# A decoder trunk's gate and up blocks: a third sum made by an accumulating transfer, another order of the products, 29 arena tiles, and norms in halves

## The chip, the core and the metric

The kernel runs on one core of a Trainium2 chip, as one program with a single launch. The metric is the device time of an execution in microseconds. TensorE (PE in the profile) multiplies, VectorE (DVE), ScalarE (ACT) and GpSimd (POOL) do elementwise work, SyncE (SP) issues loads. The times of three runs are given, and one further execution was taken with the hardware profiler.

## The reference

A trunk of two layers on `x` of 512 tokens and 1024 channels in float32. Each layer adds half a gated feed-forward network (FFN), a token mixer, and half an FFN again; a last RMS norm closes the trunk:

```python
def swiglu(h, w_gate, w_up, w_down):
    return (jax.nn.silu(h @ w_gate) * (h @ w_up)) @ w_down
...
    for layer in range(DEPTH):
        x = x + 0.5 * swiglu(rmsnorm(x, ffn_norm[layer, 0]), ffn_w_gate[layer, 0],
                             ffn_w_up[layer, 0], ffn_w_down[layer, 0])
...
        x = x + y.astype(x.dtype)
        x = x + 0.5 * swiglu(rmsnorm(x, ffn_norm[layer, 1]), ffn_w_gate[layer, 1],
                             ffn_w_up[layer, 1], ffn_w_down[layer, 1])
    return rmsnorm(x, final_norm)
```

`y` is latent attention in the first layer and an mLSTM in the second. An FFN takes 1024 channels to 2816 and back, so four pairs of gate and up matrices are multiplied.

## The kernel before, in words

The program has six phases: `f0` (FFN), `a` (attention), `f1`, `f2`, `m` (the mLSTM), `f3`. Everything stays in SBUF; only weights are loaded.

**Products of split numbers.** Every float32 operand is written as the sum of a high and a low part in the format that TensorE multiplies at full speed, and a product takes three matmuls: high by high, high by low, low by high. A weight tile of 128 x 1024 (512 KB) is split by two instructions: ACT casts it to `whi` (L161), DVE subtracts that from it to get `wlo` (L162). There are three buffers each of `whi` and `wlo`; `weights` splits up to AHEAD = 2 tiles ahead of the product that asks for one.

**A gate and up stage.** The 22 column blocks of an FFN's gate and up matrices are taken in pairs. The first NB = 2 pairs are multiplied directly (`plain`, L193 to L195). The other nine pairs, the blocks of this document, go through `seven`: a two-by-two scheme in which seven products of half-size operands do the work of eight. Its products are numbered 1 to 7. Each has a weight tile of its own, made from the four quarters a11, a12, a21, a22: product 1 takes a11, product 5 takes S1 = a22 + a21, product 6 takes s2 = a11 + S1, product 7 takes s3 = a21 + a11, product 2 takes a12, product 3 takes s4 = s2 + a12, product 4 takes a22. (The layout stores the quarters with signs so that all of these are sums.) The other operand, `b1h`, `b1l` to `b7h`, `b7l`, is made from the normed activations once a stage (`normed_blocks`). A product is 24 matmuls (L440 to L442) into one of the banks `px`, `py`, `pz`, `pw`. DVE and ACT combine the banks to `u2`, `u4`, `c12` and apply the gate (`finish`).

**How the sums are made before.** S1 and s3 are made by two transfers: SP loads one quarter (L122), then POOL issues a transfer that adds the other quarter onto the tile as it lands (L125). S1 lies in a tile of the arena, a pool of ARENA = 28 tiles of 128 x 1024 that also holds the operands `b1h` to `b7l`, the activations `act` and the `slab` tiles; s3 lies in one of three `raw` tiles. s2 and s4 are made by DVE at L149: s2 = a11 + S1 into a new arena tile, then, once s2 has been split, s4 = a12 + s2 into the same tile. a12 also has an arena tile.

**What sets the order.** `plan_ffn` writes down the order of the weight tiles, `load_later` the order of the loads. A tile's load is issued up to LOADS = 3 ahead in that list (`load_ahead`), and it waits until a buffer of its pool is free. Each engine runs its instructions in program order; the sum for the next block's s2 stands between DVE's other work wherever `value` is called for it.

**Behind the stage.** `down_plain` and `down_seven` multiply by `w_down` in the same ways; there a12 is already added by a transfer onto a sum that has been split (L166). At the end of `down_seven` eight `norm_tile` calls square each tile of `x` (ACT, L256) and add the squares (DVE, L257); in the last FFN TensorE sums them over the partitions (`rstd`, L263). `mlstm` interleaves the products of eight heads with the chain that makes their normalisers (`factors`, the `rows` matmuls at L199).

Of the kernel before, what the change touches and what calls it, by code (L numbers as in the profile page):

```python
# [26 lines left out]
F32 = mybir.dt.float32  # L27
# [7 lines left out]
P = 128  # L35
T = 512
# [8 lines left out]
DC = 3  # L45
ARENA = 28
LOADS = 3
# [17 lines left out]
class Trunk:  # L65
# [73 lines left out]
    def value(self, src):  # L139

        if src[0] == "load":
            self.first = max(self.first, src[1] + 1)
            self.load_to(self.first)
            return self.loaded[src[1]]
        if src[1] not in self.made:
            _, n, a, b, new = src[:5]
            a, b = self.value(a), self.value(b)
            t = self.duo("sum", F32) if new else b
            self.nc.vector.tensor_tensor(out=t, in0=a, in1=b, op=ALU.add)  # L149
            self.made[n] = t  # L150
        return self.made[src[1]]

    def split_pieces(self, pieces, ahead=True):
# [6 lines left out]
        for a, b in pieces or [(0, n)]:  # L160
# [3 lines left out]
            yield  # L164
        if src[0] == "sum" and len(src) == 6:
            self.nc.gpsimd.dma_start(out=raw, in_=self.row(*src[5]), accum_op=ALU.add)  # L166
        if ahead:
# [77 lines left out]
    def norm_tile(self, d):  # L245
# [3 lines left out]
        self.norm_square(d)  # L249

    def square(self, acc, src, first):
        if first:
            self.nc.scalar.activation(acc, src, AF.Square)
        else:
            sq = self.t512("sq")
            self.nc.scalar.activation(sq, src, AF.Square)  # L256
            self.nc.vector.tensor_tensor(out=acc, in0=acc, in1=sq, op=ALU.add)  # L257

    def rstd(self, acc, n, times=None):

        st = self.ps2.tile([P, T], F32, name="st", tag="st")
        for q in range(NT):
            self.nc.tensor.matmul(st[:, q:q + 1], acc[:, q * P:(q + 1) * P], self.ones[:, 0:1], start=True, stop=True)  # L263
        ms = self.small.tile([P, NT], F32, name="ms", tag="ms")
# [30 lines left out]
    def begin(self, gcol):  # L295
# [16 lines left out]
        self.ident = cst[:, 0:P]  # L312
        self.ones = cst[:, P:2 * P]
        self.mask = cst[:, 2 * P:3 * P]
        self.maskT = cst[:, 3 * P:4 * P]
        self.invf = cst[:, 4 * P:4 * P + 1]
        self.sign = cst[:, 4 * P + 1:4 * P + 2]
        self.sel = cst[:, 4 * P + 2:4 * P + 10]
        self.norm_begin(gcol)
# [14 lines left out]
    def constants(self):  # L334
        nc = self.nc
        self.onesr = self.const.tile([P, P], F32R, name="onesr")
        nc.scalar.copy(out=self.onesr, in_=self.ones)
        self.pick = self.const.tile([P, P + 40], F32R, name="pick")
# [16 lines left out]
    def normed_blocks(self, rb):  # L355
# [26 lines left out]
        t3 = self.duo("t3", F32)  # L382
        v.tensor_tensor(out=t3, in0=b22, in1=b12, op=ALU.subtract)
        v.tensor_tensor(out=b12, in0=b11, in1=b12, op=ALU.subtract)
        yield
        v.tensor_tensor(out=b11, in0=t3, in1=b11, op=ALU.add)
        split(6, b11)
        yield
        split(5, b12)
        yield  # L390
        split(7, t3)
        yield
# [32 lines left out]
    def seven(self, outs):  # L425
# [25 lines left out]
        u2 = self.t512("u2")  # L451
        nc.scalar.copy(out=u2, in_=bx)
        product(by, 6, True, True)
        v.tensor_tensor(out=u2, in0=u2, in1=by, op=ALU.subtract)
        product(bz, 5, True, False)
        u4 = self.t512("u4")
        v.tensor_tensor(out=u4, in0=u2, in1=bz, op=ALU.add)
        product(bw, 7, True, False)
        v.scalar_tensor_tensor(out=u4, in0=bw, scalar=-1.0, in1=u4, op0=ALU.mult, op1=ALU.subtract)  # L459
# [103 lines left out]
    def down_seven(self, slabs):  # L563
# [64 lines left out]
        for c in range(4):  # L628
            product(bw, 4, c, first=False)
        add(1, 0, bw, -0.5)  # L630
        for d in range(4, 8):
            self.norm_tile(d)

    def plan_ffn(self, f):
# [4 lines left out]
        for j in range(NU - NB):  # L639
            a11, a21, a22, a12 = (("wgs", f, j, i) for i in range(4))  # L640
            s1 = self.load_later(a22, pool="sum", plus=a21)
            b11 = self.load_later(a11)
            s3 = self.load_later(a21, plus=a11)
            a11 = b11
            a12 = self.load_later(a12, pool="raw")
            a22 = self.load_later(a22)
            n = 2 * (f * NU + j)
            s2 = "sum", n, a11, s1, True
            s4 = "sum", n + 1, a12, s2, False
            for p, src in ((1, a11), (6, s2), (5, s1), (7, s3), (2, a12), (3, s4), (4, a22)):  # L650
                self.plan(("st", p), W, src)
# [4 lines left out]
        for c in range(5):  # L656
            if c < 4:
                a11, a21, a22, a12 = (("wds", f, i, c) for i in range(4))
                s1 = self.load_later(a22, pool="sum", plus=a21)
                a11 = self.load_later(a11)  # L660
                sums.append(("sum", ("dn", f, c), a11, s1, True, a12))
                for p, src in ((1, a11), (6, sums[c]), (5, s1)):
                    self.plan(("dn", p), W, src)
            if c:
                self.plan(("dn", 3), W, ("sum", ("dn", f, c - 1)))
        for c in range(4):
# [273 lines left out]
    def mlstm(self, next_gain):  # L940
# [255 lines left out]
        def out(part, i):  # L1196
            self.mix_out("wo2", part, i, ys)
# [15 lines left out]
        for p in range(3):  # L1213
# [13 lines left out]
            if p == 0:  # L1227
                for f in pending:
                    f()
            decay(a + 2)  # L1230
            if p == 2:
                for f in pending:
                    f()
            conv(p + 2) if p < 2 else out(0, 0)
            decay(b + 2)
# [101 lines left out]
def layout(i):  # L1337
# [60 lines left out]
    sel = np.concatenate([np.eye(32, 8), np.eye(96, 8)]).astype(np.float32)  # L1398
    a["cst"] = c(np.concatenate([ident, ones, later, later.T, invf, sign, sel], 1))
    return a  # L1400
# [20 lines left out]
```

## Time and profile before

| what | value |
|---|---|
| median of three runs | 1874.31 us (1873.33 to 1880.12) |
| the profiled execution's own time | 1876.21 us |
| its span, in which the rows below lie | 1874.4 us |
| TensorE, busy | 1821.4 us, 12240 matmuls |
| DVE, busy | 1457.4 us |
| ACT, busy | 932.2 us |
| POOL, busy | 131.3 us |
| moved from HBM | 261.68 MB, 141 GB/s over the span |

All rows come from the profiled execution. A row of a timeline begins with its start and its length in us; `L149` is a line of the kernel, `out<-in` gives the program's names, and brackets hold the idle time ahead of an instruction and what ended it. A DMA row is the issue of a transfer; how long it takes to land is given apart.

### The profile page before, as it was taken

How to read it: one execution, taken by the hardware profiler on the slowest of the kernel's cores; microseconds unless marked ns; L12 is line 12 of the kernel's file. 1: busy time of each engine (PE TensorE's matmuls, PEld its weight loads, DVE VectorE, ACT ScalarE, POOL GpSimd, SP SyncE). 2: the span in 40 equal slices, each digit the busy share in tenths (PEclk: the TensorE clock that was granted, in tenths of full speed). 3: DMA queues.
4: the chain of work that ended last, by engine and by line, in shares of the span. 5: the costliest groups of instructions: out<-in, count | busy, mean ns of one | idle time of the engine just before them, and what ended most of it. 6: DMA issues, size and time to landing. Idle time of an engine off the chain costs nothing.

```text
span 1874.4 us, 30014 instructions
## 1 busy us (share of the span) xinstructions
PE 1821.4 (97%) x12240; PEld 1668.1 (89%) x12240; DVE 1457.4 (78%) x1903; ACT 932.2 (50%) x1312; POOL 131.3 (7%) x154
## 2 busy tenths in 40 slices
PE   9999999999999999999999999999998999999996
PEld 7999989978887999889989998997876779999896
DVE  7867799767767777788697769778878778777885
ACT  5444445566544444435444445446767544444452
POOL 1000001000000010001000000100000000000010
PEclk9999999999999999999999999999998999999998
DMA  6575667321124585577467564743221246755762
GB/s 202 146 207 141 166 185 176 129 84 63 46 69 134 148 218 144 135 189 169 135 167 204 146 178 152 185 127 113 79 68 56 68 125 162 220 137 147 197 161 91
DMA packets 74922, 265.73 MB, mean 142 GB/s; under 512 B 8336, under 2 KB 9360, under 8 KB 74784
## 3 DMA queue, kind: packets, MB, share of 16 engines
q1 hardware_dynamic: 57312, 200.30, 31.5%
q0 software_dynamic: 17472, 63.51, 19.4%
q8 instruction: 96, 1.57, 0.3%
q14 instruction: 42, 0.34, 0.1%
HBM read 261.68 MB, written 2.10 MB: 141 GB/s over the span
## 4 chain that ended last, share of the span: by engine, by line
PE 70%; DVE 9%; issue 8%; DMA 8%; ACT 3%; POOL 1%; POOLq 0%; DVEq 0%; SPq 0%; ACTq 0%
DMA sum<-in_wgs 7%; PE y L193 4%; PE y L194 4%; PE y L195 4%; PE pw L442 3%; PE pw L440 3%; PE pw L441 3%; PE pz L442 3%; PE pz L440 3%; PE pz L441 3%; PE px L440 3%; PE px L441 3%; PE px L442 3%; DVE wlo L162 2%; PE py L442 1%
## 5 line engine op out<-in xcount | busy, mean ns | idle before, releaser
L161 ACT CAST whi<-raw 128x1024 fp32r<-128x1024 f32 (+2 forms) x314 | 322.0, 1027 | 401.5 <-issue 100.1
L162 DVE TENSOR_TENSOR wlo<-raw,whi 128x1024 fp32r<-128x1024 f32 (+2 forms) x314 | 374.5, 1193 | 94.9 <-ACT whi L161 93.5
L161 ACT CAST whi<-sum 128x1024 fp32r<-128x1024 f32 x172 | 179.7, 1047 | 237.3 <-PE pz L441 74.6
L162 DVE TENSOR_TENSOR wlo<-sum,whi 128x1024 fp32r<-128x1024 f32 x172 | 209.8, 1220 | 58.6 <-ACT whi L161 58.2
L149 DVE TENSOR_TENSOR sum<-raw,sum 128x1024 f32<-128x1024 f32 x88 | 107.2, 1219 | 68.5 <-DMA sum<-in_wgs 57.2
L440 PE MATMUL pw<-b4h,whi 128*128 128x256 f32 x288 | 83.0, 288 | 6.3 <-DVE u L459 6.3
L442 PE MATMUL pw<-b4h,wlo 128*128 128x256 f32 x288 | 83.2, 289 | 4.4 <-DVE wlo L162 4.4
L442 PE MATMUL pz<-b3h,wlo 128*128 128x256 f32 x288 | 82.0, 285 | 5.2 <-DVE wlo L162 5.2
L440 PE MATMUL py<-b6h,whi 128*128 128x256 f32 x288 | 82.6, 287 | 3.0 <-ACT whi L161 3.0
L442 PE MATMUL py<-b6h,wlo 128*128 128x256 f32 x288 | 82.8, 287 | 2.4 <-DVE wlo L162 2.3
L441 PE MATMUL pw<-b4l,whi 128*128 128x256 f32 x288 | 82.6, 287 | 0.0
L441 PE MATMUL py<-b6l,whi 128*128 128x256 f32 x288 | 82.5, 286 | 0.0
L441 PE MATMUL pz<-b3l,whi 128*128 128x256 f32 x288 | 82.0, 285 | 0.0
L440 PE MATMUL pz<-b3h,whi 128*128 128x256 f32 x288 | 81.9, 284 | 0.0
L441 PE MATMUL pz<-b5l,whi 128*128 128x256 f32 x288 | 81.5, 283 | 0.0
L441 PE MATMUL px<-b1l,whi 128*128 128x256 f32 x288 | 81.4, 283 | 0.0
L441 PE MATMUL px<-b2l,whi 128*128 128x256 f32 x288 | 81.3, 282 | 0.0
L441 PE MATMUL pw<-b7l,whi 128*128 128x256 f32 x288 | 81.3, 282 | 0.0
L440 PE MATMUL px<-b1h,whi 128*128 128x256 f32 x288 | 81.3, 282 | 0.0
L440 PE MATMUL pz<-b5h,whi 128*128 128x256 f32 x288 | 81.3, 282 | 0.0
L440 PE MATMUL pw<-b7h,whi 128*128 128x256 f32 x288 | 81.2, 282 | 0.0
L440 PE MATMUL px<-b2h,whi 128*128 128x256 f32 x288 | 81.2, 282 | 0.0
(419 smaller groups left out, 6116.4 us busy)
## 6 DMA issues: line engine op xcount, KB each, us to landing
raw<-in_wgs SPq DMA_DIRECT2D x144, 512.0 KB, 4.2
sum<-in_wds POOLq DMA_DIRECT2D x48, 512.0 KB, 6.7
raw<-in_wds SPq DMA_DIRECT2D x48, 512.0 KB, 3.3
sum<-in_wgs SPq DMA_DIRECT2D x36, 512.0 KB, 4.8
sum<-in_wgs POOLq DMA_DIRECT2D x36, 512.0 KB, 6.4
raw<-in_wgs POOLq DMA_DIRECT2D x36, 512.0 KB, 5.9
sum<-in_wds SPq DMA_DIRECT2D x32, 512.0 KB, 4.5
raw<-in_wgc SPq DMA_DIRECT2D x30, 512.0 KB, 3.3
```

The source lines that it names most:

```text
L149: self.nc.vector.tensor_tensor(out=t, in0=a, in1=b, op=ALU.add)
L161: self.nc.scalar.copy(out=hi[:, a:b], in_=raw[:, a:b])
L162: self.nc.vector.tensor_tensor(out=lo[:, a:b], in0=raw[:, a:b], in1=hi[:, a:b].bitcast(F32), op=ALU.subtract)
L193: mm(out, lhs[0], rhs[0], start=start, stop=False)
L194: mm(out, lhs[0], rhs[1], start=False, stop=False)
L195: mm(out, lhs[1], rhs[0], start=False, stop=stop)
L440: mm(out, wh, bh[:, b], start=first and e + k == 0, stop=False, skip_group_check=True)
L441: mm(out, wh, bl[:, b], start=False, stop=False, skip_group_check=True)
L442: mm(out, wl, bh[:, b], start=False, stop=last and e + k == 4, skip_group_check=True)
```

## The change

- In the nine blocks of a gate and up stage s4 is no longer made by DVE. a12 is loaded into a `raw` tile, for product 2 alone; when s2 has been split, POOL issues a transfer that adds a12 from HBM onto the tile of s2 (L167 of the kernel after). A stage has nine more accumulating transfers of 512 KB and nine fewer sums on DVE.
- The order of the products is 1, 7, 6, 5, 2, 3, 4 instead of 1, 6, 5, 7, 2, 3, 4; `normed_blocks` makes the operand of product 7 earlier to match.
- A block uses two tiles of the arena (S1 and s2) and four of the `raw` loads; ARENA is 29. The constants lose their 128 columns of ones, of which one is kept and broadcast.
- The last four norm tiles of each FFN are done in halves of 256 columns: the second half, whose part of `x` is final earlier, inside the loop of product 4; the first half behind it.
- In `mlstm`, for the last pair of heads but one, the first output product is put ahead of the pending squares.

The core of the diff:

```diff
-ARENA = 28
+ARENA = 29
...
         if src[1] not in self.made:
-            _, n, a, b, new = src[:5]
+            _, n, a, b, _ = src
             a, b = self.value(a), self.value(b)
-            t = self.duo("sum", F32) if new else b
+            t = self.duo("sum", F32)
             self.nc.vector.tensor_tensor(out=t, in0=a, in1=b, op=ALU.add)
...
-        if src[0] == "sum" and len(src) == 6:
-            self.nc.gpsimd.dma_start(out=raw, in_=self.row(*src[5]), accum_op=ALU.add)
+        if src[0] == "sum" and len(src) > 2:
+            self.nc.gpsimd.dma_start(out=raw, in_=self.row(*src[4]), accum_op=ALU.add)
...
+    def norm_half(self, d, n):
+
+        t = slice(n * T // 2, n * T // 2 + T // 2)
+        if self.gcol is not None:
+            if self.xg[d] is None:
+                self.xg[d] = self.pair()
+            self.split_to([a[:, t] for a in self.xg[d]], self.x[d][:, t], self.vec(self.gcol + d))
+        self.square(self.acc[:, t], self.x[d][:, t], False)
...
         product(bx, 1, True, False)
         u2 = self.t512("u2")
         nc.scalar.copy(out=u2, in_=bx)
+        product(bw, 7, True, False)
         product(by, 6, True, True)
         v.tensor_tensor(out=u2, in0=u2, in1=by, op=ALU.subtract)
         product(bz, 5, True, False)
         u4 = self.t512("u4")
         v.tensor_tensor(out=u4, in0=u2, in1=bz, op=ALU.add)
-        product(bw, 7, True, False)
...
         for c in range(4):
             product(bw, 4, c, first=False)
+            self.norm_half(4 + c, 1)
         add(1, 0, bw, -0.5)
         for d in range(4, 8):
-            self.norm_tile(d)
+            self.norm_half(d, 0)
...
-            a12 = self.load_later(a12, pool="raw")
-            a22 = self.load_later(a22)
-            n = 2 * (f * NU + j)
-            s2 = "sum", n, a11, s1, True
-            s4 = "sum", n + 1, a12, s2, False
-            for p, src in ((1, a11), (6, s2), (5, s1), (7, s3), (2, a12), (3, s4), (4, a22)):
+            s2 = "sum", ("gu", f, j), a11, s1, a12
+            a12, a22 = self.load_later(a12), self.load_later(a22)
+            for p, src in ((1, a11), (7, s3), (6, s2), (5, s1), (2, a12), (3, s2[:2]), (4, a22)):
                 self.plan(("st", p), W, src)
...
+            conv(p + 2) if p < 2 else out(0, 0)
             if p == 2:
                 for f in pending:
                     f()
-            conv(p + 2) if p < 2 else out(0, 0)
             decay(b + 2)
```

Three places show what the change does to the order of instructions. Lines move by one here and there: the sum at L149 is L150 after the change, the subtraction at L162 is L163, the accumulation at L166 is L167.

**First, DVE in the eighth block of an FFN, where the sum for the ninth block's s2 stands** (`sum_2446` before, `sum_2482` after; its second operand is S1 of the ninth block). Before:

```order
L454 TENSOR_TENSOR u2_2276<-u2_2276,py_2245 128x512
L162 TENSOR_TENSOR wlo_2311<-raw_2177,whi_2310 128x1024
L457 TENSOR_TENSOR u4_2340<-u2_2276,pz_2246 128x512
L162 TENSOR_TENSOR wlo_2344<-sum_2210,whi_2343 128x1024
L149 TENSOR_TENSOR sum_2446<-raw_2314,sum_2282 128x1024
L459 SCALAR_TENSOR_TENSOR u4_2340<-pw_2247,u4_2340 128x512
L162 TENSOR_TENSOR wlo_2376<-raw_2179,whi_2375 128x1024
L447 TENSOR_TENSOR slab_1771<-sg_2372,u4_2340 128x256
```

After:

```order
L476 SCALAR_TENSOR_TENSOR u2_2044<-pw_2012,u2_2044 128x512
L163 TENSOR_TENSOR wlo_2252<-sum_2249,whi_2251 128x1024
L455 TENSOR_TENSOR slab_1771<-sg_2242,u2_2044 128x256
L150 TENSOR_TENSOR sum_2482<-raw_2314,sum_2214 128x1024
L163 TENSOR_TENSOR wlo_2283<-sum_1978,whi_2282 128x1024
L163 TENSOR_TENSOR wlo_2311<-raw_2177,whi_2310 128x1024
L463 TENSOR_TENSOR u2_2280<-u2_2280,py_2246 128x512
L163 TENSOR_TENSOR wlo_2342<-sum_2249,whi_2341 128x1024
```

The sum stood behind the split of the eighth block's product 3, just ahead of the `u4` that reads product 7; it now stands behind the end of the seventh block, ahead of the split of the eighth block's product 5.

**Second, DVE at the start of the third block** (the sum for its s2 is `sum_1024` before and `sum_1063` after, the split of product 6 is `wlo_1027` and `wlo_1066`). Before:

```order
L447 TENSOR_TENSOR slab_819<-sg_1021,c12_1019 128x256
L149 TENSOR_TENSOR sum_1024<-raw_892,sum_860 128x1024
L468 SCALAR_TENSOR_TENSOR u2_854<-pw_825,u2_854 128x512
L162 TENSOR_TENSOR wlo_1027<-sum_1024,whi_1026 128x1024
L447 TENSOR_TENSOR slab_820<-sg_1055,u2_854 128x256
L162 TENSOR_TENSOR wlo_1063<-sum_860,whi_1062 128x1024
L149 TENSOR_TENSOR sum_1024<-raw_991,sum_1024 128x1024
```

After:

```order
L163 TENSOR_TENSOR wlo_1023<-raw_957,whi_1022 128x1024
L455 TENSOR_TENSOR slab_820<-sg_1019,c12_1017 128x256
L476 SCALAR_TENSOR_TENSOR u2_858<-pw_826,u2_858 128x512
L455 TENSOR_TENSOR slab_821<-sg_1056,u2_858 128x256
L150 TENSOR_TENSOR sum_1063<-raw_892,sum_788 128x1024
L163 TENSOR_TENSOR wlo_1066<-sum_1063,whi_1065 128x1024
L163 TENSOR_TENSOR wlo_1097<-sum_788,whi_1096 128x1024
L163 TENSOR_TENSOR wlo_1125<-raw_991,whi_1124 128x1024
```

The second sum (`raw_991` is a12) is gone. The split of product 7 (`wlo_1023`) has come ahead, and the sum for s2 stands behind all work of the block before, directly ahead of the split of s2; the seventh block reads the same, while in most other blocks the sum stands a block earlier.

**Third, POOL's queue from the third block on** (`raw` is s3, `sum` on L125 is S1, on L167 s2 becoming s4). Before:

```order
L125 DMA raw_957<-in_wgs 128x1024
L125 DMA sum_1096<-in_wgs 128x1024
L125 DMA raw_1193<-in_wgs 128x1024
L125 DMA sum_1332<-in_wgs 128x1024
L125 DMA sum_1568<-in_wgs 128x1024
L125 DMA raw_1429<-in_wgs 128x1024
```

After:

```order
L125 DMA raw_957<-in_wgs 128x1024
L125 DMA sum_1028<-in_wgs 128x1024
L167 DMA sum_1063<-in_wgs 128x1024
L125 DMA sum_1264<-in_wgs 128x1024
L125 DMA sum_1500<-in_wgs 128x1024
L125 DMA raw_1193<-in_wgs 128x1024
L167 DMA sum_1299<-in_wgs 128x1024
L125 DMA sum_1736<-in_wgs 128x1024
```

Both begin with s3 of the third block and S1 of the fourth. Before, s3 of the fourth follows; after, s4 of the third block, then S1 of the fifth and of the sixth, and only then s3 of the fourth.

## Rows read from the trace of the kernel before

**Rows 1.** The page, part 1: busy time, share of the span, instructions of each engine.

```profile
PE 1821.4 (97%) x12240; PEld 1668.1 (89%) x12240; DVE 1457.4 (78%) x1903; ACT 932.2 (50%) x1312; POOL 131.3 (7%) x154
```

**Rows 2.** Stretches (us from:to, length, busy per engine, TensorE clock, DMA share): gate/up, one block.

```profile
55.30:249.05 193.75, 185.96 (x1513) 184.53 (x1512) 147.84 (x173) 89.00 (x116) 14.31 (x18) 0.98 0.60 160
610.90:804.20 193.30, 186.21 (x1514) 184.80 (x1513) 148.30 (x174) 88.92 (x115) 13.62 (x16) 0.98 0.61 162
965.80:1153.20 187.40, 183.95 (x1513) 183.13 (x1512) 146.55 (x172) 88.81 (x115) 13.62 (x16) 0.99 0.62 167
1554.00:1740.10 186.10, 183.09 (x1514) 181.83 (x1513) 146.59 (x172) 88.44 (x115) 13.62 (x16) 1.00 0.62 167
1006.53:1026.69 20.16, 20.16 (x171) 20.16 (x169) 16.43 (x21) 10.02 (x13) 2.55 (x3) 1.00 0.86 240
```

**Rows 3.** What TensorE waited for: us in total, times, longest.

```profile
PE pw L440 <- DVE u L459: 6.3, 6, 2.3
PE rows L199 <- ACT pr L205: 5.3, 4, 2.9
PE pz L442 <- DVE wlo L162: 5.2, 2, 3.5
PE pw L442 <- DVE wlo L162: 4.4, 8, 0.6
PE st L263 <- DVE acc L257: 3.9, 1, 3.9
...
PE py L440 <- ACT whi L161: 3.0, 3, 1.6
...
PE py L442 <- DVE wlo L162: 2.3, 3, 0.8
```

**Rows 4.** Timeline of the eighth block of f2, all engines: start us, us, engine, line, operation.

```profile
1112.04 0.33 SPq L122 DMA_DIRECT2D sum<-in_wgs  x1
...
1115.93 0.85 POOL L125 DMA_DIRECT2D sum<-in_wgs  x1 [18.03 <-DMA sum<-in_wgs]
...
1125.80 1.22 DVE L149 TENSOR_TENSOR sum<-raw,sum 128x1024 f32<-128x1024 f32 x1 [6.75 <-DMA sum<-in_wgs]
```

**Rows 5.** Stretch of 4 us after the wait in the same block.

```profile
1129.00:1133.00 4.00, 4.00 (x22) 4.00 (x22) 4.00 (x7) 1.64 (x4) 0.00 (x0) 0.57 0.66 201
```

**Rows 6.** Groups by line and shape: count, busy us, mean ns, idle before and releasers.

```profile
L161 ACT CAST whi<-sum 128x1024 fp32r<-128x1024 f32 x172 | 179.7, 1047 | 237.3 <-PE pz L441 74.6 <-issue 40.2 <-PE dx L582 20.2
L149 DVE TENSOR_TENSOR sum<-raw,sum 128x1024 f32<-128x1024 f32 x88 | 107.2, 1219 | 68.5 <-DMA sum<-in_wgs 57.2 <-PE y L194 8.0 <-DMA raw<-in_wgs 3.3
...
L257 DVE TENSOR_TENSOR acc<-acc,sq 128x512 f32<-128x512 f32 x53 | 36.3, 685 | 1.7 <-ACT sq L256 1.1
...
L447 DVE TENSOR_TENSOR slab<-sg,u 128x256 f32<-128x256 f32 x64 | 26.7, 418 | 4.8 <-ACT sg L446 4.8
```

**Rows 7.** Line 166, the accumulations onto a split sum in the down stage.

```profile
  ACT whi L161: 14.7, 3
...
DMA to landing us min/median/max: 5.3/6.3/8.9
```

**Rows 8.** Line 125, the accumulations behind a load.

```profile
DMA to landing us min/median/max: 5.2/6.6/9.8
```

**Rows 9.** The page, part 6, loads of the seven-blocks: count, KB each, us to landing.

```profile
raw<-in_wgs SPq DMA_DIRECT2D x144, 512.0 KB, 4.2
```

**Rows 10.** The page, part 3, the two queues (SP's q1, POOL's q0): packets, MB, share.

```profile
q1 hardware_dynamic: 57312, 200.30, 31.5%
q0 software_dynamic: 17472, 63.51, 19.4%
```

**Rows 11.** Timeline of DVE at the first block of f0.

```profile
57.58 1.22 DVE L149 TENSOR_TENSOR sum<-raw,sum 128x1024 f32<-128x1024 f32 x1
58.72 0.68 DVE L420 TENSOR_TENSOR gr<-g,rb 128x512 f32<-128x512 f32 x1
```

**Rows 12.** Timeline of DVE behind the last product.

```profile
1856.61 3.08 DVE L257 TENSOR_TENSOR acc<-acc,sq 128x512 f32<-128x512 f32 x4
```

More of the change, by code (lines that the diff above doesn't have):

```diff
@@ L254, in square @@
         else:
-            sq = self.t512("sq")
+            sq = self.t512("sq")[:, :src.shape[1]]
             self.nc.scalar.activation(sq, src, AF.Square)
@@ L262, in rstd @@
         for q in range(NT):
-            self.nc.tensor.matmul(st[:, q:q + 1], acc[:, q * P:(q + 1) * P], self.ones[:, 0:1], start=True, stop=True)
+            self.nc.tensor.matmul(st[:, q:q + 1], acc[:, q * P:(q + 1) * P], self.one, start=True, stop=True)
         ms = self.small.tile([P, NT], F32, name="ms", tag="ms")
@@ L312, in begin @@
         self.ident = cst[:, 0:P]
[L313 to L318, printed above, removed]
+        self.mask = cst[:, P:2 * P]
+        self.maskT = cst[:, 2 * P:3 * P]
+        self.invf, self.sign, self.one = (cst[:, 3 * P + i:3 * P + i + 1] for i in range(3))
+        self.sel = cst[:, 3 * P + 3:3 * P + 11]
         self.norm_begin(gcol)
@@ L336, in constants @@
         self.onesr = self.const.tile([P, P], F32R, name="onesr")
-        nc.scalar.copy(out=self.onesr, in_=self.ones)
+        nc.scalar.copy(out=self.onesr, in_=self.one.broadcast_to([P, P]))
         self.pick = self.const.tile([P, P + 40], F32R, name="pick")
@@ L383, in normed_blocks @@
         v.tensor_tensor(out=t3, in0=b22, in1=b12, op=ALU.subtract)
+        split(7, t3)
+        yield
         v.tensor_tensor(out=b12, in0=b11, in1=b12, op=ALU.subtract)
+        v.tensor_tensor(out=b11, in0=t3, in1=b11, op=ALU.add)
         yield
-        v.tensor_tensor(out=b11, in0=t3, in1=b11, op=ALU.add)
         split(6, b11)
@@ L389, in normed_blocks @@
         split(5, b12)
-        yield
-        split(7, t3)
         yield
@@ L660, in plan_ffn @@
                 a11 = self.load_later(a11)
-                sums.append(("sum", ("dn", f, c), a11, s1, True, a12))
+                sums.append(("sum", ("dn", f, c), a11, s1, a12))
                 for p, src in ((1, a11), (6, sums[c]), (5, s1)):
@@ L664, in plan_ffn @@
             if c:
-                self.plan(("dn", 3), W, ("sum", ("dn", f, c - 1)))
+                self.plan(("dn", 3), W, sums[c - 1][:2])
         for c in range(4):
@@ L1398, in layout @@
     sel = np.concatenate([np.eye(32, 8), np.eye(96, 8)]).astype(np.float32)
-    a["cst"] = c(np.concatenate([ident, ones, later, later.T, invf, sign, sel], 1))
+    a["cst"] = c(np.concatenate([ident, later, later.T, invf, sign, ones[:, :1], sel], 1))
     return a
```

## The prediction, made before the changed kernel was run

> **What bounds the kernel now.** I read the page first, then busy time and clock by stretch, then the waits of the matmul engine, and last the timeline around a few of these waits. TensorE is busy 97% of the span [rows 1], so time can come only from its idle stretches or from stretches at a lower clock. The change works in the four gate and up stages. Nine blocks of seven products stand in each, and a block in which nothing waits takes 20.16 us, 2.88 a product (the last of [rows 2]). Undisturbed, the four stages would take 4 x 9 x 20.16 = 725.8 us; they take 193.75 + 193.30 + 187.40 + 186.10 = 760.6. So **34.8 us** are lost there, and the parts of the change that lie in these stages cannot win more.
>
> What the loss consists of is in TensorE's waits [rows 3]: `pw` on DVE's `u`, `pz` on `wlo` and `pw` on `wlo` make 6.3 + 5.2 + 4.4 = 15.9 us; `py` on `whi` and on `wlo`, 3.0 + 2.3 = 5.3, is the first block of a stage. The rest, about 13.6, is the lower of the two clock levels (1.2 instead of 2.4 GHz) behind such waits and what the waits' records leave out: the stretch after one of them was granted 0.57 over 4 us, so it cost 4 x 0.43 = 1.7 [rows 5].
>
> Why the 15.9 arise is seen in the eighth block of f2 [rows 4]. S1 of the ninth is loaded from 1112.04, POOL issues what is added to it at 1115.93, and the sum at L149, which needs the result, starts only at 1125.80, after DVE has idled 6.75 us. DVE works in order: behind that sum stands the `u` of product 7 (first order excerpt), and TensorE's `pw` waits for it. DVE idles 57.2 us in the whole kernel for such sums [rows 6], most of it hidden.
>
> **The change, part by part.**
>
> *Earlier S1.* A block holds two arena tiles instead of three, and there are 29 instead of 28, so S1 is loaded and accumulated one to two blocks earlier in the queues (third order excerpt). Both S1 terms, the 15.9 of waits and some 7 of the clock behind them, should go. The sum for the ninth block now stands at the start of the eighth, ahead of the split of product 5 (first order excerpt); a late a11 could hold it there, but product 5 is fourth and has slack.
>
> *The DVE sum that goes.* 36 x 1.219 = 43.9 us of DVE work [rows 6] disappear. DVE is at 78% [rows 1], so by itself this is worth nothing; it gives slack to the splits.
>
> *The accumulation that comes.* s4 = s2 + a12 must be made between the end of s2's split and the start of product 3's. Product 3 is sixth and starts 14.4 us into a block; its split has to start about 2 us earlier (a cast of 1.05 and a subtraction as long as the sum, 1.22 [rows 6], less the 0.24 until the third matmul), near 12.35. In an ordinary block s2's split is over 2.3 to 4.5 us into the block (a cast and a subtraction, with up to two more DVE operations ahead), which leaves 8 to 10 us. In the third and seventh block the sum stands late on DVE (second order excerpt), s2's split ends one sum and one or two short operations later, at 5.5 to 6.8, and 5.6 to 6.8 are left. The same kind of accumulation, on a split sum in the down stage, landed in 5.3, 6.3 and 8.9 us (least, median, most), and ACT's cast waited 14.7 us for three of them [rows 7]; those at L125 took 5.2, 6.6 and 9.8 [rows 8]. Per place the cost lies between 0 and 9.8 - 5.6 = 4.2; I take **1.5**, a landing between the median and the most, as these places fall where loads are dense: 8 x 1.5 = 12 us.
>
> The Trainium skill, page "DMA: Bandwidth & Descriptors", section "Anatomy of one DMA — SWDGE (gpsimd) path", fits a transfer issued from GpSimd by 2.0 us + bytes / 436e3, an estimate of 3.2 us for these 512 KB. By it the third sum would be in time in every block, and the time that of rival B. The trace disagrees for accumulating transfers: none landed under 5.2 us [rows 8], and I keep the rows.
>
> *s3 earlier in the block.* Product 7 is now second, and its raw tile is one of four loads a block that share three buffers: the load waits for the split of the previous block's product 2, which begins with the third product, 5.8 us into that block, and is over at about 8.6. The split of 7 has to start by 20.16 + 2.88 + 0.24 - 1.05 - 1.22 = 21.0. So load and accumulation have 12.4 us; the medians need 4.2 [rows 9] + 6.6 [rows 8] = 10.8. I take 0, and count the delay of the fourth block (its accumulation stands behind two of S1, third order excerpt) among the 8 places above. At the top of the rows, 4.2 + 9.8 = 14.0, it would be 1.6 in each of 32 blocks, 51 us.
>
> *The DMA engines.* A plain load keeps all 16 engines busy for 0.315 x 1874.4 / (200.30 / 0.524) = 1.55 us, an accumulating one for 0.194 x 1874.4 / (63.51 / 0.524) = 3.0 [rows 10]. A block had 5 loads and 2 accumulations, 13.7 us; it now has 5 and 3, 16.7 of 20.16: 0.15 more than a share that is 0.60 to 0.62 now [rows 2]. The last block of [rows 2] ran at a share of 0.86 with no wait, so I expect longer landings but no saturation. POOL's own 36 x 0.85 us [rows 4] change nothing at 7% busy.
>
> *The first block of a stage.* Product 6, which waits for a late sum, gets 2.88 us more. But the subtraction for product 7 comes ahead of it on DVE (1.14 from start to start), and so do the two products with `rb`, which stood behind the sum (1.2) [rows 11]. In f0 the sum then runs from 57.58 + 2.34 = 59.9 to 61.1, the cast and the subtraction end at 63.4, and the third matmul of product 6, due at 55.3 + 2 x 2.88 + 0.24 = 61.3, is 2.1 late; before it was some 0.8 more. So 0.8 goes in each of the three stages that wait, and 5.3 - 2.4 = 2.9 stay.
>
> *Norms in halves.* Behind the last product, four squares and adds are half as long. The adds took 3.08 us together [rows 12]; like the ones of 128x256, at 418 instead of 685 ns [rows 6], four take 1.7, and the first square is some 0.2 shorter: **-1.6** in the tail, where `st` waits 3.9 for them [rows 3]. In the other FFNs nothing is listed as waiting for this chain: 0. The other halves lie under product 4.
>
> *The reordered lines of the mLSTM.* The longest wait of `rows` on ACT, 2.9 [rows 3], stands ahead of what moves; -0.3, between 0 and -1. The smaller `cst` and the copy of a broadcast column: 0, under the first loads; some tenths without that cover.
>
> **Sum.** The stages lose 2.9 + 12 + four low-clock stretches of 1.7 (6.8) = 21.7 instead of 34.8: -13.1. With -1.6 and -0.3 this is -15.0. The profiled execution took 1876.2 us, so 1861.2; it lies 1.9 above the median of the three runs, 1874.3, which makes **1859** as the median.
>
> **The rivals.** *B: all of it comes.* Landings stay near 6.6 and no block but the first waits: 2.9 + two low-clock stretches (3.4) = 6.3 lost, -28.5 and -1.9, so 1844. For it speaks the block at 0.86; against it, the 14.7 us that the twin of this accumulation cost the down stage. *C: the waits move.* Little is won if the late sums are met by landings of 8.9, against 6.2 of time: 2.7 x 8 = 21.6, + 2.9 + 6.8 = 31.3 lost, so about 1869; should S1's loads be held by arena tiles after all, so that the change does not do what it says, nearly nothing is won, 1872. *D, slower: s3 is the new bottleneck.* Three accumulations a block share one queue and slow each other; product 7, now second, waits for the one of s3 in most blocks. It decides from 12.4 us on; at 14.0 it costs 51, so the stages lose 51 + 2.9 + 6.8 = 60.7 against 34.8, and the median is 1898. From about 13.5 on (1.1 in each of 32 blocks) the kernel is measurably slower. For it speaks that the accumulation issued at 1115.93, with plain loads beside it, was not in until 1125.8 [rows 4]; against it the median of 6.6.
>
> **How the numbers follow.** About 0.5% of 1874, 9.4 us, can be told from no change. Forecast 0.50 (its own range 1850 to 1868), B 0.10, C 0.22, D 0.18. Faster: 0.43 of the forecast and B, 0.53. Same: the rest of the forecast and most of C, 0.27. Slower: D and a little of C, 0.20. The range takes in B's and C's times and the beginning of D: 1844 to 1886.
>
> **What would show it.** Right: the sum's wait for `sum<-in_wgs` falls from 57 us to under 10; the stages take about 187 us each; TensorE's wait of `pw` for `u` is gone; the new waits are those of `pz` for `whi` or `wlo`, behind accumulations of a12, in the third and seventh block; `st` waits about 2.3. Wrong: `pw` of product 7 waits for its split in many blocks, at DMA shares near 0.9 (D); accumulations of a12 land near 6 and nothing waits for them (B). I would be wrong in kind if DVE still idles for S1.

## The result, and the profile after

The changed kernel is slower: 1936.39 us in the median (1924.75 to 1942.42, 4 runs) against 1877.21 for the kernel before (1873.33 to 1881.25, 4 runs), a ratio of **1.0308** with the 95% interval 1.0247 to 1.0368. The forecast was 1859, the range ended at 1886. Its profiled execution took 1942.4 us, the slowest of the four and 6 us above their median, with a span of 1940.6.

The page, parts 1 and 3, of the kernel after, beside [rows 1, 10]:

```profile
PE 1848.5 (95%) x12240; PEld 1690.5 (87%) x12240; DVE 1416.7 (73%) x1895; ACT 930.6 (48%) x1340; POOL 163.1 (8%) x190
...
q1 hardware_dynamic: 57312, 200.30, 29.5%
q0 software_dynamic: 22640, 82.32, 24.4%
```

DVE is busy 41 us less (36 sums fewer, some short norm halves more) and POOL's queue carries 18.8 MB more, as the diff says. The four gate and up stages, beside [rows 2]:

```profile
55.55:264.20 208.65, 191.60 (x1514) 189.25 (x1513) 139.87 (x166) 88.59 (x116) 22.73 (x27) 0.96 0.69 177
628.70:835.00 206.30, 190.40 (x1513) 188.07 (x1512) 139.82 (x166) 88.72 (x117) 22.27 (x26) 0.97 0.70 179
996.00:1203.05 207.05, 192.83 (x1513) 189.54 (x1512) 138.81 (x165) 86.87 (x115) 22.19 (x26) 0.96 0.69 178
1603.75:1808.90 205.15, 190.16 (x1514) 187.69 (x1513) 140.60 (x167) 88.87 (x117) 22.17 (x26) 0.97 0.71 182
```

They sum to 827.2 us, 101.4 above the 725.8 of undisturbed blocks, where the kernel before lost 34.8. The difference, 66.6, is the whole difference of the two spans (66.2). The DMA share rose by 0.07 to 0.09 only. What TensorE waited for, beside [rows 3]:

```profile
PE pz L448 <- DVE u L466: 24.5, 13, 3.8
PE pw L448 <- ACT whi L162: 13.2, 8, 3.5
PE py L448 <- ACT whi L162: 8.4, 4, 2.9
PE pw L450 <- DVE wlo L163: 7.3, 10, 0.8
PE pz L448 <- ACT whi L162: 5.8, 6, 3.2
...
PE st L273 <- DVE acc L267: 2.8, 1, 2.8
PE py L450 <- DVE wlo L163: 2.3, 4, 1.5
```

The `pw` that waited for `u` is gone, as forecast; in its place stand `pz` (product 3), `pw` on a split (product 7) and a longer `py` (product 6 of the first block). Who is late is seen in the waits of ACT and DVE:

```profile
ACT whi L162 <- DMA raw<-in_wgs: 145.5, 33, 9.0
ACT whi L162 <- DMA sum<-in_wgs: 120.7, 24, 8.3
...
DVE sum L150 <- DMA raw<-in_wgs: 33.4, 18, 4.0
```

DVE's sum no longer waits for S1 at all (57.2 us before [rows 6]). ACT's cast now waits 33 times for an accumulated s3 and 24 times for an accumulated s4. From the starts of the products in the trace (2.88 us apart when undisturbed) the 101.4 divide thus, the stretches at the lower clock behind a wait included (the granted clock of the stages is 0.96 to 0.97, before 0.98 to 1.00): about 43 ahead of product 3 (s4), 36 ahead of product 7 (s3), 18 in the first blocks, 4 elsewhere.

**One late s4.** The third block of f1 began at 675.5. Timelines of POOL, then DVE, ACT and TensorE:

```profile
677.68 0.85 POOL L125 DMA_DIRECT2D sum<-in_wgs  x1 [8.47 <-DMA sum<-in_wgs]
681.79 0.86 POOL L167 DMA_DIRECT2D sum<-in_wgs  x1 [3.27 <-DMA sum<-in_wgs]
682.33 1.19 POOL L125 DMA_DIRECT2D sum<-in_wgs  x1
...
692.01 1.23 DVE L163 TENSOR_TENSOR wlo<-sum,whi 128x1024 fp32r<-128x1024 f32 x1 [3.22 <-ACT whi L162]
693.15 0.68 DVE L466 TENSOR_TENSOR u<-u,pz 128x512 f32<-128x512 f32 x1
...
690.93 1.04 ACT L162 CAST whi<-sum 128x1024 fp32r<-128x1024 f32 x1 [8.31 <-DMA sum<-in_wgs]
...
693.98 0.36 PE L448 MATMUL pz<-b3h,whi 128*128 128x256 f32 x1 [3.77 <-DVE u L466]
```

The accumulation of a12 was issued 6.3 us into the block, between two for S1, and took until 690.83. The cast, the subtraction and then the `u` at L466 follow; only then does TensorE go on, 3.77 us late. L466 reads product 5 out of the bank that product 3 adds to. Product 5 is now fourth instead of third, and DVE's order has that read **behind** the split of product 3:

```
L463 TENSOR_TENSOR u2_1094<-u2_1094,py_1060 128x512
L163 TENSOR_TENSOR wlo_1156<-sum_1063,whi_1155 128x1024
L466 TENSOR_TENSOR u4_1183<-u2_1094,pz_1061 128x512
```

Before, the same read (L457) stood ahead of `wlo`. So a late s4 costs the time of the split and of this read as well.

**One late s3.** Timelines of SP, POOL and ACT around the start of the fifth block of f1:

```profile
711.21 17.57 SPq L122 DMA_DIRECT2D raw<-in_wgs  x4
...
716.98 0.85 POOL L125 DMA_DIRECT2D raw<-in_wgs  x1 [6.67 <-DVE slab L455]
...
726.12 1.04 ACT L162 CAST whi<-raw 128x1024 fp32r<-128x1024 f32 x1 [8.93 <-DMA raw<-in_wgs]
```

The load is issued 9.9 us into the fourth block (which began at 701.3) and lands in 5.2, POOL follows 0.6 later, and the accumulation takes 9.0: 14.8 us, where the prediction had 12.4 to spend.

**The first block.** ACT and DVE in f1:

```profile
627.15 1.05 ACT L162 CAST whi<-raw 128x1024 fp32r<-128x1024 f32 x1 [5.04 <-DMA raw<-in_wgs]
...
628.24 1.23 DVE L163 TENSOR_TENSOR wlo<-raw,whi 128x1024 fp32r<-128x1024 f32 x1 [2.87 <-ACT whi L162]
```

The subtraction of product 7 stands ahead of everything else on DVE and waits 2.87 us for s3 (2.99 in f2, 2.78 in f3, 0.72 in f0); a subtraction and three splits for the operands, the two products with `rb`, the sum and the split of product 6 stand behind it. TensorE's product 6 came 2.90 us late.

The tail did what it should; DVE and TensorE behind the last product, beside [rows 3, 12]:

```profile
1924.22 2.00 DVE L267 TENSOR_TENSOR acc<-acc,sq 128x256 f32<-128x256 f32 x4
...
1926.37 1.79 PE L273 MATMUL st<-cst,acc 128*128 128x1 f32 x8 [2.79 <-DVE acc L267]
```

### The profile page after: what moved, and what is told of

Its sections match the earlier page's. It is cut to its first block, busy times and chain, and to the rows that moved or that the text cites. A ratio compares the mean times of both kernels' runs of the same rounds, so it can differ in the third digit from the quotient of the medians.

```text
span 1940.6 us, 30163 instructions
## 1 busy us (share of the span) xinstructions
PE 1848.5 (95%) x12240; PEld 1690.5 (87%) x12240; DVE 1416.7 (73%) x1895; ACT 930.6 (48%) x1340; POOL 163.1 (8%) x190
## 5 line engine op out<-in xcount | busy, mean ns | idle before, releaser
L162 ACT CAST whi<-raw 128x1024 fp32r<-128x1024 f32 (+2 forms) x314 | 321.5, 1025 | 432.4 <-DMA raw<-in_wgs 145.5
L163 DVE TENSOR_TENSOR wlo<-raw,whi 128x1024 fp32r<-128x1024 f32 (+2 forms) x314 | 374.2, 1193 | 192.8 <-ACT whi L162 192.0
L162 ACT CAST whi<-sum 128x1024 fp32r<-128x1024 f32 x172 | 179.1, 1045 | 293.6 <-DMA sum<-in_wgs 120.7
L163 DVE TENSOR_TENSOR wlo<-sum,whi 128x1024 fp32r<-128x1024 f32 x172 | 209.2, 1220 | 123.5 <-ACT whi L162 123.3
L448 PE MATMUL pz<-b3h,whi 128*128 128x256 f32 x288 | 87.1, 302 | 28.9 <-DVE u L466 24.5
L448 PE MATMUL pw<-b7h,whi 128*128 128x256 f32 x288 | 86.6, 301 | 13.2 <-ACT whi L162 13.2
L450 PE MATMUL pw<-b7h,wlo 128*128 128x256 f32 x288 | 87.0, 302 | 7.3 <-DVE wlo L163 7.3
L150 DVE TENSOR_TENSOR sum<-raw,sum 128x1024 f32<-128x1024 f32 x52 | 63.4, 1220 | 37.8 <-DMA raw<-in_wgs 33.4
L448 PEld LDWEIGHTS pz<-b3h,whi 128*128 128x128 f32 x288 | 58.9, 204 | 32.0 <-issue 27.1
L449 PE MATMUL pw<-b7l,whi 128*128 128x256 f32 x288 | 85.2, 296 | 0.0
L450 PE MATMUL pz<-b5h,wlo 128*128 128x256 f32 x288 | 81.6, 283 | 0.4 <-DVE wlo L163 0.4
L450 PE MATMUL px<-b1h,wlo 128*128 128x256 f32 x288 | 81.2, 282 | 0.0
```

The lines of the kernel that those rows point to most:

```text
L162: self.nc.scalar.copy(out=hi[:, a:b], in_=raw[:, a:b])
L163: self.nc.vector.tensor_tensor(out=lo[:, a:b], in0=raw[:, a:b], in1=hi[:, a:b].bitcast(F32), op=ALU.subtract)
L448: mm(out, wh, bh[:, b], start=first and e + k == 0, stop=False, skip_group_check=True)
L449: mm(out, wh, bl[:, b], start=False, stop=False, skip_group_check=True)
L450: mm(out, wl, bh[:, b], start=False, stop=last and e + k == 4, skip_group_check=True)
```

## The experiments

Theory A: the place of product 7 is at fault, that is, the order of the products. Theory B: the third accumulation overloads the DMA queues. Theory C: S1's loads, now ahead in bursts, delay s4. "Lost" below is the time of the four gate and up stages above 725.8 us in each run's profile; ratios are to the kernel before in the same session. The kernel before itself took 1877 us (median) in the session of the change, 1884 in that of experiments 1 to 4, 1882 in that of 5 to 8, 1879 in that of 9 to 11 and 1883 in that of 12.

**1. The old order, all else as changed.** The three places (the products in `seven`, the plan, the operands) go back:

```diff
...
-            for p, src in ((1, a11), (7, s3), (6, s2), (5, s1), (2, a12), (3, s2[:2]), (4, a22)):
+            for p, src in ((1, a11), (6, s2), (5, s1), (7, s3), (2, a12), (3, s2[:2]), (4, a22)):
...
```

> The changed kernel with the products in the old order 1, 6, 5, 7, 2, 3, 4; the third accumulation and the 29 tiles stay. In the profile of the change the four gate and up stages lose 101 us: about 42 where product 3 waits for s4, 36 where product 7 waits for s3, 24 in the first blocks. Theory A (the place of product 7 is at fault: s3's load and accumulation have 12.4 us, and its split stalls DVE's queue in the first block): s3 gets 5.8 us more, s4 2.9 more, so the stages lose 20 to 35 and the time is 1865 to 1880. Theory B (the third accumulation overloads the DMA queues): the transfers are still there, product 3 and product 7 still wait, 60 us or more are lost, 1900 to 1930.

Measured: **0.9872** (0.9836 to 0.9907), 1862.84 us in the median; 23.9 us lost. That is 1.3% faster than the kernel before, with the third accumulation in place. The stages, then rows of the waits of DVE and ACT (ACT's for s4 stood at 120.7 us, its for s3 at 145.5 and is gone), then TensorE's longest wait in the blocks:

```profile
54.10:243.05 188.95, 183.97 (x1514) 183.13 (x1513) 142.40 (x167) 90.32 (x117) 21.90 (x26) 0.99 0.75 194
605.90:794.85 188.95, 183.91 (x1514) 183.09 (x1513) 141.40 (x166) 89.77 (x116) 21.40 (x25) 0.99 0.75 194
955.85:1140.55 184.70, 182.22 (x1513) 181.57 (x1512) 139.66 (x164) 89.69 (x116) 21.36 (x25) 1.00 0.77 198
1540.80:1727.95 187.15, 183.95 (x1513) 183.12 (x1512) 141.17 (x166) 89.86 (x116) 21.37 (x25) 0.99 0.76 195
```

```profile
DVE sum L150 <- DMA sum<-in_wgs: 33.1, 8, 5.5
...
ACT whi L162 <- DMA sum<-in_wgs: 9.9, 4, 3.7
```

```profile
PE pz L450 <- DVE wlo L163: 10.2, 8, 2.6
```

The DMA share is higher than in the change (0.75 to 0.77), as the same transfers fill less time, and nothing waits for s3. s4 is issued 0.05 us ahead of its block in the median (6.5 into it in the change), so that every s4 has landed by 11.5 us into its block. B falls as the whole cause. What remains are 10.2 us in the first blocks and eight waits of product 3 in the third and seventh blocks, 13.7 us with the clock behind them, all from DVE's sum that still waits for S1 there.

**2. The new order with DVE's sum for s4**, so without the third accumulations:

```diff
...
+            s4 = "sum", ("g4", f, j), a12, s2
-            for p, src in ((1, a11), (7, s3), (6, s2), (5, s1), (2, a12), (3, s2[:2]), (4, a22)):
+            for p, src in ((1, a11), (7, s3), (6, s2), (5, s1), (2, a12), (3, s4), (4, a22)):
...
```

> The changed kernel with s4 made by DVE again (a12 in its raw tile added onto s2's tile), in the new order and with 29 tiles, so without the 36 third accumulations. Theory A: product 7 still waits for s3 and the first blocks are as in the change, the waits of product 3 go: 50 to 60 us lost, 1890 to 1905. Theory B: without the third accumulation loads and accumulations land as before, s3 is in time, 15 to 30 us are lost, 1860 to 1875.

Measured: 1.0089 (1.0058 to 1.0121), 71.8 us lost. The order alone makes the kernel slower than before; the waits for s3 are all there without any third accumulation:

```profile
ACT whi L162 <- DMA raw<-in_wgs: 156.6, 31, 10.2
```

The loss was larger than theory A had put it (50 to 60): product 7 costs about 41 us, 24 of them in the fourth blocks (10 in the change), and about 9 lie at products 6 and 5.

**3. Both undone**, so that only the earlier S1 is left of the change in the stages:

```diff
...
+            s4 = "sum", ("g4", f, j), a12, s2
-            for p, src in ((1, a11), (7, s3), (6, s2), (5, s1), (2, a12), (3, s2[:2]), (4, a22)):
+            for p, src in ((1, a11), (6, s2), (5, s1), (7, s3), (2, a12), (3, s4), (4, a22)):
...
```

> Old order and DVE's sum for s4 both back: what stays of the change in these stages is two arena tiles a block of 29 and a12 in a raw tile, so that S1 is loaded earlier, besides the norm halves and the reordered lines of the mLSTM. If S1's lateness was the cause of the 24 us that the kernel before loses behind its sums (both theories): these go, first blocks lose 10, 10 to 15 in all, 1850 to 1857. If the early S1 only moves the waits to s3 (four raw loads share three tiles): 1870 to 1885.

Measured: 0.994 (0.9916 to 0.9964), 36.0 us lost in a profiled execution of 1876.1 us. The S1 waits did not go: they are the same kind as before, in the third and seventh blocks, and a few of product 5 came, behind sums that wait for a12 or a11; nothing waits for s3. So the third accumulation, in the old order, is what makes 36.0 into 23.9. What is left of the change here loses as much in its profile as the kernel before did in an execution of 1876.2 us, while the ratio makes it 0.6% faster than the kernel before in its own session; what the earlier S1 is worth alone stays open.

**4. The change with 28 tiles.**

```diff
-ARENA = 29
+ARENA = 28
```

> The changed kernel with 28 arena tiles instead of 29, all else as changed. Theory C (S1's loads running two blocks ahead come in a burst at the third and seventh block and delay s4 there): the waits of product 3 in the third and seventh blocks shrink from about 3 us to 1 or less, 1915 to 1925. Theories A and B: S1 is only a little later, the same waits stay, 1930 to 1945.

Measured: 1.0245 (1.0212 to 1.0279), 91.4 us lost. The waits ahead of product 3 did not shrink (TensorE's `pz` on `u`: 36.4 us in 15 cases, 24.5 in 13 in the change). This does not settle theory C, as the edit leaves S1 almost where it was: POOL's queue has the same order in all four stages as in the change, S1 of the fourth block ahead of s4 of the third, S1 of the fifth and sixth ahead of s3 of the fourth. POOL in the third block of f1 (from 669.1):

```profile
670.98 0.85 POOL L125 DMA_DIRECT2D sum<-in_wgs  x1 [8.17 <-DMA sum<-in_wgs]
675.59 0.86 POOL L167 DMA_DIRECT2D sum<-in_wgs  x1 [3.76 <-DVE wlo L163]
676.17 1.15 POOL L125 DMA_DIRECT2D sum<-in_wgs  x1
```

For theory C speaks the first experiment, where S1 of the fourth block comes behind s4 of the third (from 648.2), and S1 of the fifth behind s3 of the fourth:

```profile
650.99 0.85 POOL L167 DMA_DIRECT2D sum<-in_wgs  x1 [8.62 <-DVE wlo L163]
654.82 0.86 POOL L125 DMA_DIRECT2D sum<-in_wgs  x1 [2.98 <-DMA sum<-in_wgs]
```

There s4 of the third and seventh blocks landed in 5.4 us in the median (8.2 in the change), and s3 of the fourth and eighth in 5.3 (7.7). So a part of the loss may lie in S1's earlier place in the queues, which the new order brings with it; no run moved S1 alone, and this stays open.

**5. The kernel before with the norm halves and the mLSTM lines alone.**

```diff
...
             product(bw, 4, c, first=False)
+            self.norm_half(4 + c, 1)
         add(1, 0, bw, -0.5)
         for d in range(4, 8):
-            self.norm_tile(d)
+            self.norm_half(d, 0)
...
```

> The kernel before with only the norm halves and the reordered lines of the mLSTM. The prediction put these at -1.6 and -0.3, a ratio to the kernel before of 0.999; TensorE's wait for the last add falls from 3.9 to about 2.8 us, as it did in the profile of the change. If the halves' extra instructions cost something in the other three FFNs: 1.000 or above.

Measured: 1.000 (0.9983 to 1.0017). TensorE's wait for the last add is 2.8 us instead of 3.9 there too; 1.1 us is less than this comparison can show.

**6. Product 7 third.**

```diff
...
-            for p, src in ((1, a11), (7, s3), (6, s2), (5, s1), (2, a12), (3, s2[:2]), (4, a22)):
+            for p, src in ((1, a11), (6, s2), (7, s3), (5, s1), (2, a12), (3, s2[:2]), (4, a22)):
...
```

> The changed kernel with product 7 third (1, 6, 7, 5, 2, 3, 4), the third accumulation and 29 tiles kept: between the old order, in which nothing waited for s3, and the new one. s3's chain gets 2.9 us more than in the change: 15.3 instead of 12.4. Theory A (a deadline that s3's chain of load, queue and accumulation misses by 1 to 4 us): most of s3's waits go, s4's stay near the 14 us of the old order or a little more, 30 to 50 us are lost in the stages, ratio 0.995 to 1.005. If instead product 7 has to be behind product 5 for another reason (the queue order of DVE), the loss stays near that of the change, ratio 1.02 or more.

Measured: 1.0057 (1.0037 to 1.0077), 55.2 us lost, at or just past the slow edge of what theory A gave. It is between the two orders, but less for s3 than for product 3: product 7 costs about 15 us of these, product 3 about 33. In 15 blocks product 3 starts about 1 us or more late (5.1 at most): product 5 is fourth here too, and the read of `pz` stands behind a split that is late itself, behind a late s4 or behind a sum that waits for S1 or a11. The run also shows two accumulations issued one right behind the other, for S1 and for s4, in f2:

```profile
996.01 0.85 POOL L125 DMA_DIRECT2D sum<-in_wgs  x1 [7.60 <-DMA sum<-in_wgs]
996.55 1.19 POOL L167 DMA_DIRECT2D sum<-in_wgs  x1
```

The first landed after 6.6 us, the second after 10.7.

**7. The change with four raw buffers** and 28 tiles.

```diff
-ARENA = 29
+ARENA = 28
...
-        raw = self.duo(pool, F32) if pool else self.wp.tile([P, W], F32, name="raw", tag="raw")
+        raw = self.duo(pool, F32) if pool else self.wp.tile([P, W], F32, name="raw", tag="raw", bufs=4)
```

(One more raw load is allowed ahead, too.)

> The changed kernel, its new order and third accumulation kept, with four raw buffers instead of three and 28 arena tiles (the run with 28 tiles and three buffers is the base: ratio 1.0245). If s3 is late because its load waits for the buffer of a12, it can now start one split earlier or more, and the waits of product 7 go: ratio 1.00 to 1.01. If it is late because the accumulations land late whenever they are issued: 1.02 or more.

Measured: 1.0155 (1.0124 to 1.0186) against 1.0245 with three buffers, between the two expectations; 72.1 us lost against 91.4. s3's load is issued 9 us earlier, and only two casts still wait for an s3, 2.0 us in all; no product 7 does. That its load waited for the buffer of a12 is shown. But the accumulations of s4 still land 12.1 us into their block in the median (12.7 with three buffers), each now taking 6.8 us instead of 5.5, and product 3 waits 44 us instead of 40:

```profile
PE pz L448 <- DVE u L466: 36.1, 17, 3.8
PE pz L448 <- ACT whi L162: 8.0, 7, 2.0
```

**8. The old order with product 3 last.**

```diff
...
-            for p, src in ((1, a11), (7, s3), (6, s2), (5, s1), (2, a12), (3, s2[:2]), (4, a22)):
+            for p, src in ((1, a11), (6, s2), (5, s1), (7, s3), (2, a12), (4, a22), (3, s2[:2])):
```

> The old order but with product 3 last (1, 6, 5, 7, 2, 4, 3), third accumulation and 29 tiles kept. In the old order with product 3 sixth, eight waits of product 3 for s4 in the third and seventh blocks cost 13.7 us in all. s4 now has 2.9 us more: these waits fall to below 3 us in all unless they move to the next block's first products, 10 us of first blocks stay: 12 to 15 us lost in the stages, ratio 0.980 to 0.984. If s4's landing was not the deadline that was missed: no change, 0.987.

Measured: 0.9965 (0.9944 to 0.9986), 39.8 us lost; a miss. The eight waits did not go but moved to product 4: DVE's sum that waits for S1 stands ahead of the `u` that reads product 7's bank, to which product 4 adds, one product sooner. So in the old order it was not s4 that was late.

**9. The change with product 3 last.**

```diff
...
-            for p, src in ((1, a11), (7, s3), (6, s2), (5, s1), (2, a12), (3, s2[:2]), (4, a22)):
+            for p, src in ((1, a11), (7, s3), (6, s2), (5, s1), (2, a12), (4, a22), (3, s2[:2])):
```

> The changed kernel with product 3 last instead of sixth (1, 7, 6, 5, 2, 4, 3), all else as changed. In its profile s4 had landed 13.2 us into a block in the median, and 20 of 36 came after 12.3, where the cast of product 3 should begin; the latest came at 16.9. Product 3 last puts that point to 15.2. If missing this point is what costs: the 42 us behind product 2 fall to 10 or less, the 36 for s3 and 20 in the first blocks stay, 60 to 70 us lost, ratio 1.012 to 1.018. If the waits for s4 only show what DVE, ACT or the queues are late with anyway, product 4 waits in its place and the ratio stays at 1.025 to 1.03.

Measured: 1.0231 (1.019 to 1.0273), between the two expectations; 75.0 us lost, in the fastest of its four executions. The waits behind product 2 fall to about 8 us, as the missed deadline of s4 would have it, and the first blocks cost 15 us, but product 7 costs about 44 instead of 36 and some 7 lie at product 6, so that the sum came out 5 us above what was expected. POOL's queue has the order of the change here too, and yet s4 of the third and seventh blocks landed in 5.3 us in the median: a place in the queue alone does not make it late.

**10. The old order with 28 tiles**, the edits of experiments 1 and 4 together.

> The old order with the third accumulation (the run that was fastest, ratio 0.9872) with 28 arena tiles instead of 29. If the 29th tile is what brings S1 earlier: the waits behind S1's sum in the third and seventh blocks (13.7 us with 29) grow to 20 to 25, ratio 0.992 to 0.997. If two tiles a block instead of three do that alone: 0.985 to 0.989.

Measured: 0.9932 (0.9912 to 0.9952), 1863.78 us in the median, 23.7 us lost, as much as with 29. The ratios differ by half a per cent, but the kernel's own times hardly (1862.84 and 1861.99 with 29 tiles): it is the kernel before that took 1884.25 us in the one session and 1878.83 in the other. Neither the times nor the profiles show that the 29th tile is worth anything.

**11. The old order, four raw buffers, 28 tiles**, the edits of experiments 1 and 7 together.

> The old order with the third accumulation, 28 arena tiles and four raw buffers instead of three. S1 of the fourth and eighth blocks is loaded behind a22, which waits for a raw buffer; with a fourth buffer it should come some us earlier and the 13.7 us of waits in the third and seventh blocks shrink to 5 or less: ratio 0.980 to 0.984, better than both kernels and than 29 tiles. If the earlier plain loads take the DMA engines from the accumulations, or s3's accumulation comes ahead of s4's in POOL's queue: 0.99 to 1.00.

Measured: 0.9969 (0.9947 to 0.999), 36.4 us lost; a miss. The waits stay in the third block, and product 5 of the fourth waits up to 6.3 us in f3.

**12. The first experiment again**, the same kernel, as the version that beats both:

> The run in the old order with the third accumulation and 29 tiles once more, the same kernel, with more rounds: it was 0.9872 (0.9836 to 0.9907) of the kernel before, its twin with 28 tiles 0.9932, although the two lose the same in their profiles (23.9 and 23.7 us in the stages, against 34.65 before). If the losses in the profile are right, both are 11 us faster there and 1 in the tail, a ratio of 0.993 to 0.994; if the first measurement holds, 0.987.

Measured: 0.9886 (0.9867 to 0.9906), 1861.99 us in the median; 24.5 us lost. The kernel before took 1882.74 us here. The four combinations, by what is lost in the stages of their profiles, and by their ratios:

| | DVE's sum for s4 | third accumulation |
|---|---|---|
| old order | 36.0 us, 0.9940 | 23.9 us, 0.9872 |
| new order | 71.8 us, 1.0089 | 101.4 us, 1.0308 |

The order costs 36 us without the third accumulation and 77 with it; the third accumulation saves 12 in the old order and costs 30 in the new, and the ratios go the same way. So theory A holds as far as the order goes, and B holds where the order has left the transfers no slack: the two together cost more than the sum of what each does alone. How much of the order's cost is the shorter time of s3 and how much is S1's earlier place in the queues (theory C) is not shown.

## Why the prediction was wrong, step by step

**Earlier S1: half right.** In the change DVE's sum stopped waiting for S1, and the waits that this had caused went. But experiments 1 and 3 show that the tiles alone don't do this: in the old order eight and four such waits stay. In the new order the scheduler put the load of S1 for the fourth and eighth blocks ahead of a22 of the block before in SP's queue, in the old order behind it. That this place makes the difference was not tried by itself.

**The step that failed: "s3 earlier in the block ... I take 0."** The 12.4 us that load and accumulation have was the right frame. The medians of the rows before, 4.2 + 6.6 = 10.8, were the wrong filling: they were taken where nothing hurried. Three terms were missing. The load starts 9.0 us into the block in the median (8.6 was taken). It starts up to 9.9 in where the block is not late itself, because the split that frees its buffer stands on DVE behind the sum, which waits for a11 (the 33.4 us above; the prediction saw this wait and gave it slack), and up to 16.8 in a block whose own product 7 is late. POOL issues 0.6 us after the load lands. And in the fourth and eighth blocks, where accumulations of S1 stand ahead in POOL's queue, the load itself takes up to 10.1 and the accumulation up to 9.3, together 13 to 20. It cost 36 us, the clock behind the waits included, instead of 0. Rival D had the mechanism, with 51 and a chance of 0.18; its 1898 was still 38 us short, as it had no more than the forecast for the first blocks and nothing for s4.

**"The accumulation that comes": right place, too few places, wrong point.** In the third and seventh blocks s4 was issued 6.3 us into the block, as reckoned (5.5 to 6.8), and landed in 8.2 instead of the 7.7 taken. But the point to meet was not the split alone: the read of `pz` behind it adds 0.7 us and more. And the other blocks, given 8 to 10 us, issue s4 at 6.7 in the median, not at 2.3 to 4.5: behind a late product 7 all that follows is late, and the sixth blocks are late without one (5.5 to 8.1). It cost 43 us, with the clock, instead of 12 and a share of the 6.8 for the clock. In the old order it cost nothing.

**"The first block": wrong sign.** The working left out that the subtraction of product 7 can itself wait, for s3, and holds DVE's queue. The waits of `py` are 10.7 us, in place of 5.3 before and 2.9 forecast; with the clock behind them the first blocks cost 18.

**Norms in halves and the mLSTM:** -1.1 in place of -1.6, and the wait of `rows` on ACT is the same 2.85 as before: nothing.

**The DMA engines:** no saturation in the mean of a stage, as said; the version that works runs at 0.75 to 0.77, and single stretches of the change reach 0.94 (below). The Trainium skill, page "DMA: Bandwidth & Descriptors", section "Anatomy of one DMA — SWDGE (gpsimd) path", would have had these transfers land in 3.2 us (an estimate from its fit); none of those at L167 did so in under 5.2, so the rows were rightly kept.

Taken without the new order, the sum stands near what was measured: 21.7 us lost were forecast, 23.9 were found in the first experiment's profile, and a ratio of 0.992 (1859 to 1874.3) stands against 0.987 and 0.989. That is luck, as the parts differ: first blocks 10.2 with the clock for 2.9 without, S1 13.7 for 0, s4 0 for 12, and the forecast was not made for that order. What was misjudged is the order of the products: the sum priced the move of one product, and not what stands behind it in three queues, nor what the scheduler moves along with it.

## What to carry to other kernels

When a step is moved earlier, count its whole chain (the event that frees its buffer, the load, the issue, the accumulation) at the durations of the busiest blocks, and follow each in-order engine past it: what waits there now holds everything behind. When a change bundles a new way of making an operand with a new order, run all four combinations: here the new way saves 12 us in the one order and costs 30 in the other. Before a run counts against a theory, see in the trace that its edit moved what the theory speaks of: 28 tiles left POOL's queue as it was. A read that must come between two products of one accumulating bank is a deadline of its own: look where it stands on its engine.

## What the runs showed that had not been expected

Accumulating transfers delay one another in POOL's queue. In the profile of the change the 38 of the gate and up weights that were issued while the one before was still on its way took 7.9 us to land in the median (12.1 at most), the 70 others 5.4. Before, 15 of 72 overlapped in this way, so that the median of 6.6, which also takes in 32 of the down stage, described a queue that was mostly empty. Plain loads beside them are not the whole reason: in the first experiment, of those with three plain loads under way beside them, 25 that were alone in the queue took 5.4 us and 25 that overlapped 7.5. Many plain loads cost time as well; in the change the eight that were alone with four or five took 8.1. Landings at L167 and L125 of the change:

```profile
DMA to landing us min/median/max: 5.2/6.0/9.5
```

```profile
DMA to landing us min/median/max: 5.2/6.0/12.1
```

Both medians are lower than before [rows 7, 8], though the kernel waits for them: what counts is the landing of those that something waits for. A stretch of 15 us in which three of them and five plain loads were under way for most of their time shows a DMA share of 0.94:

```profile
676.00:691.00 15.00, 14.20 (x118) 13.93 (x116) 8.01 (x10) 3.91 (x6) 2.70 (x4) 1.00 0.94 262
```
